# Split-GELU-multiply on one core: VectorE's implied waits dropped, and output tiles fixed instead of rotating

## The chip, the cores and the metric

The kernel runs on 1 core of one Trainium2 chip. The metric is the device time of one execution in microseconds (us); lower is better. A run is timed as a whole; the profile covers a span of it, which is 1.8 us shorter here.

## The reference

The input `x` is float32 of shape (32, 512, 2048), which is 16,384 rows. Each row is split in halves, and the output is GELU of the first half times the second half:

```python
half_dim = x.shape[-1] // 2
x1, x2 = x[..., :half_dim], x[..., half_dim:]
gelu_x1 = 0.5 * x1 * (1 + erf(x1 / np.sqrt(2)))
return (gelu_x1 * x2).astype(np.float32)
```

134.22 MB are read and 67.11 MB written, with one GELU and one product per output element.

## The kernel before

The rows are cut into 16 tiles of 128 partitions by 8 rows. A tile of `x` takes 64 KiB of each partition and a tile of output 32 KiB. Both come from pools with two buffers each. Loads run on the sync engine's queue, two tiles ahead. ScalarE writes GELU into the output tile, VectorE multiplies it in place, and the store is issued from ScalarE's queue (those of the last two tiles from the sync engine's). The first and the last tile are cut in three pieces, the 14 others in two (5 rows and 3 rows).

```python
    xpool = ctx.enter_context(tc.tile_pool(name="xpool", bufs=2))
    opool = ctx.enter_context(tc.tile_pool(name="opool", bufs=2))
    # ... load(i) takes a tile of xpool and starts its DMA; store(...) starts a DMA out ...
    ahead = [load(0), load(1)]
    for i in range(n_tiles):
        x_tile = ahead.pop(0)
        o_tile = opool.tile([P, R, half], out.dtype, name="o_tile")
        # ... last, pieces ...
        steps = ((0, 2), (2, 4), (4, 8)) if pieces else ((0, 5), (5, 8))
        for lo, hi in steps:
            rows = slice(lo, hi)
            tc.keep_in_program_order(
                nc.scalar.activation(out=o_tile[:, rows, :], in_=x_tile[:, rows, :half], func=GELU)
            )
            nc.vector.tensor_mul(
                out=o_tile[:, rows, :], in0=o_tile[:, rows, :], in1=x_tile[:, rows, half:]
            )
            # ... stores of the first and last tile, by halves ...
        if not pieces:
            store(nc.sync if i == n_tiles - 2 else nc.scalar, i, o_tile, slice(0, R))
        if i + 2 < n_tiles:
            ahead.append(load(i + 2))
```

The semaphores are placed by the tile framework. It makes the multiply wait for everything that it depends on: the GELU, the load of `x_tile`, the store that last used the output buffer, and the multiply before that. ScalarE had to wait for the load and the store too, before it began the GELU.

Of the kernel before, what the change touches and what calls it, by code (L numbers as in the profile page):

```python
# [1 line left out]

# [4 lines left out]

GELU = mybir.ActivationFunctionType.Gelu


@with_exitstack
def kernel(
    ctx: ExitStack,
    tc: tile.TileContext,
    x: bass.AP,
    out: bass.AP,
):








    nc = tc.nc
    P = nc.NUM_PARTITIONS

    x_flat = x.flatten_outer_dims()
    out_flat = out.flatten_outer_dims()  # L30
    n_rows, dim = x_flat.shape
    half = dim // 2

    R = 8
    x_t = x_flat.rearrange("(n p r) d -> n p r d", p=P, r=R)
    o_t = out_flat.rearrange("(n p r) d -> n p r d", p=P, r=R)
    n_tiles = x_t.shape[0]

    xpool = ctx.enter_context(tc.tile_pool(name="xpool", bufs=2))
    opool = ctx.enter_context(tc.tile_pool(name="opool", bufs=2))  # L40

    def load(i):
        x_tile = xpool.tile([P, R, dim], x.dtype, name="x_tile")
        for rows in (slice(0, 4), slice(4, 8)) if i == 0 else (slice(0, 8),):
            nc.sync.dma_start(out=x_tile[:, rows, :], in_=x_t[i][:, rows, :])  # L45
        return x_tile

    def store(queue, i, o_tile, rows):
        queue.dma_start(out=o_t[i][:, rows, :], in_=o_tile[:, rows, :])

    ahead = [load(0), load(1)]
    for i in range(n_tiles):
        x_tile = ahead.pop(0)
        o_tile = opool.tile([P, R, half], out.dtype, name="o_tile")
        last = i == n_tiles - 1
        pieces = i == 0 or last
        steps = ((0, 2), (2, 4), (4, 8)) if pieces else ((0, 5), (5, 8))
        for lo, hi in steps:
            rows = slice(lo, hi)
            tc.keep_in_program_order(  # L60
                nc.scalar.activation(  # L61
                    out=o_tile[:, rows, :], in_=x_tile[:, rows, :half], func=GELU
                )
            )
            nc.vector.tensor_mul(  # L65
                out=o_tile[:, rows, :],
                in0=o_tile[:, rows, :],
                in1=x_tile[:, rows, half:],
            )
            if pieces and hi % 4 == 0:  # L70
                store(nc.sync if last else nc.scalar, i, o_tile, slice(hi - 4, hi))
        if not pieces:
            store(nc.sync if i == n_tiles - 2 else nc.scalar, i, o_tile, slice(0, R))
        if i + 2 < n_tiles:
            ahead.append(load(i + 2))


# [1 line left out]
_INS = ['x']  # L79
_OUTS = [((32, 512, 1024), 'float32')]  # L80


# [23 lines left out]
```

## Time and profile before

| What | Value |
|---|---|
| Time, median (range) of the first 3 runs | 470.94 us (470.83 to 471.09) |
| Span of the profile | 469.1 us |
| DMA rate over the span | 429 GB/s |
| VectorE busy, ScalarE busy | 30%, 25% |
| Multiplies, separate wait instructions before them | 34, 31 |

The prediction shows the main lines and reads them. The page lists for each DMA queue its packets, MB and share of 16 engines' time, and for each kind of DMA issue its count, size and median us from issue to landing:

```profile
q14 instruction: 2, 0.02, 0.0%
...
out_dram<-o_tile ACTq DMA_DIRECT2D x13, 4096.0 KB, 44.7
```

The first line says that two packets in the span carried the program's own instructions. The trace has both as 8,192 bytes, at 453.6 and 453.7 us, and 0.309 us long. The second line says that a 4 MB store takes 44.7 us to land.

### The profile page before, as it was taken

Reading aid. Unit: us, or ns where it says so; the run is one execution under the profiler, and the core shown is the slowest. Engines: PE = TensorE matmul, PEld = TensorE weight load, DVE = VectorE, ACT = ScalarE, POOL = GpSimd, SP = SyncE. Lnnn points to the kernel's source line nnn. Section 1 sums busy time; section 2 is a strip of 40 time slices with the busy share of each in tenths; the row PEclk is TensorE's granted clock in tenths of the full one; section 3 lists DMA queues with packets and bytes.
Section 4 is the critical chain, followed back from the end, with each engine's and each line's share of the span. In section 5 each row is a group of like instructions: output and inputs, shape, how many; then the busy total and the mean of one; then the engine's idle time right before and its main releaser. Section 6 shows DMA issues by size and latency. Waiting matters only on the chain.

```text
span 469.1 us, 210 instructions
## 1 busy us (share of the span) xinstructions
DVE 140.5 (30%) x34; ACT 115.5 (25%) x35; POOL 0.2 (0%) x4
## 2 busy tenths in 40 slices
DVE  0330515206051160611506025070240703407052
ACT  1420606041060410505005050140601406023060
POOL 0000000000000000000000000000000000000000
DMA  8999999999999999999999999999999999999998
GB/s 358 447 447 447 414 391 492 402 402 447 492 402 402 447 469 425 402 447 425 469 402 430 419 492 402 402 447 492 402 402 447 469 425 402 447 425 469 402 412 349
DMA packets 5042, 201.35 MB, mean 429 GB/s; under 512 B 560, under 2 KB 560, under 8 KB 560
## 3 DMA queue, kind: packets, MB, share of 16 engines
q1 hardware_dynamic: 2880, 142.61, 70.4%
q10 hardware_dynamic: 2160, 58.72, 29.0%
q14 instruction: 2, 0.02, 0.0%
HBM read 134.22 MB, written 67.11 MB: 429 GB/s over the span
## 4 chain that ended last, share of the span: by engine, by line
DMA 75%; DVE 14%; ACT 8%; ACTq 0%; issue 0%; SPq 0%
DMA out_dram<-o_tile 66%; DVE o_tile L65 14%; DMA x_tile<-in_x_dram 10%; ACT o_tile L61 8%; ACTq L101 0%; SPq L45 0%
## 5 line engine op out<-in xcount | busy, mean ns | idle before, releaser
L65 DVE TENSOR_TENSOR o_tile<-o_tile,x_tile 128x5120 f32<-128x5120 f32 (+3 forms) x34 | 140.5, 4171 | 319.9 <-ACT o_tile L61 319.9
L61 ACT ACTIVATE o_tile<-x_tile 128x5120 f32<-128x5120 f32 (+3 forms) x34 | 114.3, 3407 | 339.6 <-DMA out_dram<-o_tile 301.8
L61 ACT ACT_TABLE_LOAD x1 | 1.3, 1283 | 0.7 <-PEq L90 0.7
L90 POOL MEMSET const-bfloat16-1.0<- 128x1 bf16 x1 | 0.1, 101 | 0.0
L90 POOL MEMSET const-uint8-127<- 128x1 uint8 x1 | 0.1, 101 | 0.0
L90 POOL MEMSET const-float32-0.0<- 128x1 f32 x1 | 0.1, 98 | 0.2 <-issue 0.2
L90 POOL MEMSET const-float32-1.0<- 128x1 f32 x1 | 0.1, 98 | 0.0
## 6 DMA issues: line engine op xcount, KB each, us to landing
out_dram<-o_tile ACTq DMA_DIRECT2D x13, 4096.0 KB, 44.7
x_tile<-in_x_dram SPq DMA_DIRECT2D x2, 4096.0 KB, 16.6
out_dram<-o_tile ACTq DMA_DIRECT2D x2, 2048.0 KB, 34.5
out_dram<-o_tile SPq DMA_DIRECT2D x1, 4096.0 KB, 25.8
out_dram<-o_tile SPq DMA_DIRECT2D x2, 2048.0 KB, 8.0
x_tile<-in_x_dram SPq DMA_DIRECT2D x15, 44.5
```

Source lines behind the costliest of these rows:

```text
L61: nc.scalar.activation(out=o_tile[:, rows, :], in_=x_tile[:, rows, :half], func=GELU)
L65: nc.vector.tensor_mul(out=o_tile[:, rows, :], in0=o_tile[:, rows, :], in1=x_tile[:, rows, half:],)
L90: nc = _bacc.Bacc("TRN2", target_bir_lowering=False, num_devices=1)
```

## The change

The intent: VectorE shall wait for ScalarE alone. What ScalarE waited for before a GELU is done when that GELU is done, so the multiply behind it need not wait for it again. The framework keeps such waits, so they are declared unnecessary. Fixed output tiles make the dependency on the buffer's earlier use one that can be named and dropped; a rotating pool makes that wait itself.

```diff
-    opool = ctx.enter_context(tc.tile_pool(name="opool", bufs=2))
+    opool = ctx.enter_context(tc.tile_pool(name="opool", bufs=1))
+    o_tiles = [opool.tile([P, R, half], out.dtype, name=f"o{k}_tile") for k in range(2)]
 ...
-            nc.sync.dma_start(out=x_tile[:, rows, :], in_=x_t[i][:, rows, :])
+            dma = nc.sync.dma_start(out=x_tile[:, rows, :], in_=x_t[i][:, rows, :])
+            before_gelu[i % 2].append(dma.ins)
 ... (the same in store)
-        o_tile = opool.tile([P, R, half], out.dtype, name="o_tile")
+        o_tile = o_tiles[i % 2]
 ...
-            nc.vector.tensor_mul(
+            mul = nc.vector.tensor_mul(
                 ...
             )
+            for ins in before_gelu[i % 2]:
+                tc.declare_no_dep(mul.ins, ins, reason="ScalarE waited for it")
+            muls.append(mul.ins)
 ...
+        before_gelu[i % 2].extend(muls)
```

More of the change, by code (lines that the diff above doesn't have):

```diff
@@ L44, in load @@
         for rows in (slice(0, 4), slice(4, 8)) if i == 0 else (slice(0, 8),):
-            nc.sync.dma_start(out=x_tile[:, rows, :], in_=x_t[i][:, rows, :])
+            dma = nc.sync.dma_start(out=x_tile[:, rows, :], in_=x_t[i][:, rows, :])
+            before_gelu[i % 2].append(dma.ins)
         return x_tile
     def store(queue, i, o_tile, rows):
-        queue.dma_start(out=o_t[i][:, rows, :], in_=o_tile[:, rows, :])
+        dma = queue.dma_start(out=o_t[i][:, rows, :], in_=o_tile[:, rows, :])
+        before_gelu[i % 2].append(dma.ins)
+    before_gelu = [], []
     ahead = [load(0), load(1)]
@@ L57 @@
         steps = ((0, 2), (2, 4), (4, 8)) if pieces else ((0, 5), (5, 8))
+        muls = []
         for lo, hi in steps:
```

## The prediction

> **What bounds the kernel now.** I read the page's busy shares first, then the waits, then the chain that ended last, then the packets of the DMA queues.
>
> ```profile
> span 469.1 us, 210 instructions
> DVE 140.5 (30%) x34; ACT 115.5 (25%) x35; POOL 0.2 (0%) x4
> ...
> DMA  8999999999999999999999999999999999999998
> ...
> HBM read 134.22 MB, written 67.11 MB: 429 GB/s over the span
> ## 4 chain that ended last, share of the span: by engine, by line
> DMA 75%; DVE 14%; ACT 8%; ACTq 0%; issue 0%; SPq 0%
> ```
>
> VectorE (DVE) works for 30% of the span and ScalarE (ACT) for 25%, while the DMA row stands at 9 in every slice but the first and the last. The chain seems to say something else: it gives VectorE 14% and ScalarE 8%, as if a faster VectorE could shorten the run. It follows waits backwards, from each GELU to the store that freed its buffer, from that store to the multiply, and so on. It does not ask whether the DMA engines were working beside the compute pieces. The table of busy time by stretch does. Its columns are the stretch in us and its length, busy time and count for DVE, ACT and POOL, the clock, the DMA share and the rate; the second stretch holds eight tiles.
>
> ```profile
> 100.48:129.48 29.00, 8.76 (x2) 7.12 (x2) 0.00 (x0) 1.00 1.00 434
> 158.48:390.48 232.00, 70.09 (x16) 56.98 (x16) 0.00 (x0) 1.00 1.00 434
> ```
>
> A tile is 8 MB in and 4 MB out, 12.58 MB in decimal units, and 12.58 MB / 29.00 us = 434 GB/s. The mean DMA share over whole periods is 1.00. A single period could still hide a hole in its compute part, so I laid the packet records over the span myself, each split between the stretches it touches: 100.48 to 113.78 us, where ScalarE and VectorE work on a tile, has a share of 1.00, and 113.78 to 129.48, where both are idle, also 1.00. The first large packet starts 1.75 us into the span and the last ends at 467.77; the share is 1.00 all the way between 3 and 467 us. So **the DMA engines are the bound, with no hole in them**. A typical packet, 32,768 bytes in 1.213 us, is 27.0 GB/s on one engine and 432 GB/s on sixteen; 201.33 MB at 432 GB/s is 466.0 us, which is what lies between those two packets.
>
> **What the change touches.** It touches the waits of VectorE, so I read who waits for whom, on the engines and on the queue that issues the loads.
>
> ```profile
> DVE o_tile L65 <- ACT o_tile L61: 319.9, 18, 21.1
> ACT o_tile L61 <- DMA out_dram<-o_tile: 301.8, 14, 22.1
> ACT o_tile L61 <- DMA x_tile<-in_x_dram: 37.8, 3, 21.0
> ...
> SPq L45 <- DMA x_tile<-in_x_dram: 214.1, 14, 20.4
> SPq L45 <- DVE o_tile L65: 182.6, 14, 13.5
> ```
>
> All of VectorE's idle time, 319.9 us, ends with ScalarE's GELU; none of it ends with a DMA. The waits on DMAs are ScalarE's, 301.8 + 37.8 us. VectorE waits for these DMAs too, in separate instructions, but by the time the GELU is done they are long satisfied. The instructions of the multiply's line between 71 and 77 us show one case (count, shortest, median and longest ns, first and last start):
>
> ```profile
> L65 DVEq EVENT_SEMAPHORE  x2: 50/50/50, 71.5 to 71.6; - x2
> L65 DVE TENSOR_TENSOR o_tile<-o_tile,x_tile x1: 5493/5493/5493, 76.1 to 76.1; 128x5120 f32<-128x5120 f32 x1
> ```
>
> and the timeline around it (start, length, what, idle time before):
>
> ```profile
> 71.56 7.12 ACT L61 ACTIVATE o_tile<-x_tile 128x5120 f32<-128x5120 f32 x2 [17.31 <-DMA out_dram<-o_tile]
> 76.06 8.76 DVE L65 TENSOR_TENSOR o_tile<-o_tile,x_tile 128x5120 f32<-128x5120 f32 x2 [15.67 <-ACT o_tile L61]
> ```
>
> Both wait instructions run as the GELU starts, at 71.5 and 71.6 us, and are over at about 71.66. The multiply starts at 76.06, when the first GELU (4.47 us) has ended at 76.03. The waits have some 4.4 us to spare.
>
> **What the Trainium skill says.** (1) "Perfetto Trace Analysis", section Identifying Dependency Chains: an instruction that waits on several engines may get EventSemaphore instructions put before it for the further waits. The trace agrees: the multiply's line has 34 multiplies and 31 EVENT_SEMAPHORE, and these 31 are what the change takes out. (2) The same page, section Per-engine timelines, on a DVE or Act instruction: it is pushed into a wait queue, waits there for its semaphores, and only its execution is what the profile calls the instruction. That fits the 0.03 us between the GELU's end and the multiply's start, with the sequencer's waits already behind it. (3) "VectorE: DVE Perf Modes", The DRAIN you can't avoid: eight copies took 13.88 us with a semaphore after each and the same with one after the last alone, so semaphores between operations cost nothing there. Nothing in this trace shows a cost either: the second multiply of a tile follows the first without a gap (5.49 + 3.35 = 8.84 us of work in a span of 8.76). (4) The first page again, Roofline: a core alone is bounded by its 16 DMA engines, about 435 GB/s. The trace has 434 in the steady stretch, so no room is left there.
>
> **The change part by part.** The order of instructions and the waits of the built programs were compared engine by engine; no time is in that.
>
> Removed: the 31 EVENT_SEMAPHORE in front of multiplies (one for the first piece, for the third and for tile 1, then two for each of the 14 tiles after, 3 + 28 = 31). In the trace they take 21 or 50 ns each, at most 31 x 50 ns = 1.55 us in all. On the path that sets the end: 0, since each is done about 4.4 us (1.6 to 3.6 us for the pieces of the first and the last tile) before the GELU that the multiply needs anyway.
>
> Unchanged: the 34 multiplies, 34 GELUs and 35 DMA issues stand in the same order with the same shapes, every multiply still waits for ScalarE, ScalarE keeps all its waits for loads and stores, and the sync engine's waits before each load are the same in number and kind.
>
> Moved: the two fixed output tiles lie at the same two addresses that the rotating pool used in turn, and tile i uses buffer i mod 2 as before. Nothing is added: a buffer is refilled when its store has landed, and ScalarE still waits for that.
>
> Sum on the path: 0 from waits, 0 from buffers. Suppose against this that every removed wait had delayed its multiply by its whole length. A multiply that ends 0.1 us earlier lets the store and the load after next be issued 0.1 us earlier, behind transfers that have not finished: load 3 was issued at 60.41 us and its landing took about 44.5 us, where its 8.39 MB alone need 19.4 us at 432 GB/s. The DMA engines have no hole that the earlier issue could fill, so the gain would be spent in the queue. Only the last multiply has transfers behind it that could end earlier, and even there the last store waits behind two others: compute ends at 460.4 us, the DMA at 467.8. So 470.94 + 0 = **470.9 us**.
>
> **The rivals.** *(A) The waits do cost, tile after tile.* The chain of compute and store per buffer is closed: 13.3 us from GELU to the end of the multiplies and 44.7 us to landing make 58.0 us, two tiles' period. If the landing time were fixed, 0.071 us saved per tile (21 + 50 ns, the usual pair) would be worth about 16 x 0.071 = 1.1 us, 0.2%, and the time would be 469.8. Against it: the wait instructions run beside the GELU, and 44.7 us is a queueing time, far over the 9.7 us that 4.19 MB need. *(B) VectorE gets ahead, and earlier issues change how loads and stores mix.* If something moved by a few us, the last store could land later or earlier by some part of one 2 MB piece, which is 4.9 us at 432 GB/s; the range would be 466 to 476. For it: loads and stores share the same engines. Against it: VectorE cannot get ahead, because the GELU's semaphore is the last of its waits in all 18 cases of the waits view. *(C) The fixed buffers bring a new wait,* as when a release of the tile pool had been finer than a buffer dependency: a GELU that waited for a multiply or a store more would lengthen a tile by up to 8.8 us and the run by up to 30%. For it: a pool and a fixed tile are not tracked in the same way. Against it: the built program has the same waits on ScalarE and on the sync engine, row by row.
>
> **Range and chances.** The three runs of before spread over 0.26 us. The mean is set by the bytes and the packet rate, which the change does not touch, so I take a few times that spread for another chip and session: 470.2 to 471.6. (A) alone would fall a little below it, and I give it a tenth. Faster by over 2% would need 461.5 us, under the 466 us that the packets need: 0.01, for an error in this reading. Slower by over 2%, 480.4 us, needs (C) or something that I haven't seen: 0.01. Within 2%: 0.98.
>
> **What would show it.** Right: the EVENT_SEMAPHORE of the multiply's line are gone and the instruction count is 210 - 31 = 179; VectorE's idle time still ends with ScalarE alone, near 320 us over 18 times; the timeline repeats to some 0.05 us, with a period of 29.0 us; the steady rate is 434 GB/s. Step "the waits are hidden" is wrong if the gap between GELU's end and multiply's start falls below 0.03 us. Step "the DMA has no hole" is wrong if the period shrinks below 28.9 us. The prediction falls if ScalarE waits for something else, or if a period grows.

## The result

| Kernel | Runs | Median (range), us |
|---|---|---|
| before | 6 | 470.94 (470.79 to 471.09) |
| changed | 6 | 470.63 (470.49 to 470.87) |

The ratio is 0.9994, 95% interval 0.9981 to 1.0006: the same. Ratios here are the mean time of one kernel's fast runs over that of the other's of the same rounds, so not quite the ratio of the medians quoted.

The page of the changed kernel, with the parts that answer to those shown of before:

```profile
span 469.1 us, 179 instructions
DVE 140.5 (30%) x34; ACT 115.5 (25%) x35; POOL 0.2 (0%) x4
...
q14 instruction: 1, 0.01, 0.0%
HBM read 134.22 MB, written 67.11 MB: 429 GB/s over the span
...
DMA 75%; DVE 14%; ACT 8%; ACTq 0%; issue 0%; SPq 0%
```

The instruction count fell from 210 to 179, which is the 31 wait instructions. Busy times, rate and chain stand as before. Of the lines shown one differs otherwise: one packet of instructions instead of two, at 453.7 us. The busy time by stretch of the changed kernel, with the columns as in the prediction:

```profile
100.48:129.48 29.00, 8.76 (x2) 7.12 (x2) 0.00 (x0) 1.00 1.00 434
158.48:390.48 232.00, 70.08 (x16) 56.98 (x16) 0.00 (x0) 1.00 1.00 434
```

The rate is still 434 GB/s, and tiles take 29.0 us; the length of a stretch is chosen, so what it shows is the count of pieces and the rate. (Later in this execution single tiles take up to 29.1 us; more on that under the prediction.) Who waited for whom in the changed kernel, in total us, times and longest:

```profile
DVE o_tile L75 <- ACT o_tile L71: 320.4, 18, 20.9
ACT o_tile L71 <- DMA out_dram<-o_tile: 302.4, 14, 22.0
...
SPq L49 <- DVE o_tile L75: 182.9, 14, 13.5
```

VectorE's idle time hasn't shrunk, 320.4 us after 319.9. And its timeline at the tile that the prediction showed:

```profile
71.58 7.12 ACT L71 ACTIVATE o_tile<-x_tile 128x5120 f32<-128x5120 f32 x2 [17.37 <-DMA out_dram<-o_tile]
76.08 8.76 DVE L75 TENSOR_TENSOR o_tile<-o_tile,x_tile 128x5120 f32<-128x5120 f32 x2 [15.73 <-ACT o_tile L71]
```

The multiply starts 4.50 us after its GELU starts, as before (76.06 - 71.56). No wait instruction of the multiply's line is left there.

### The profile page after: what moved, and what is told of

It reads as the page before. It is cut to its first block, busy times and chain, and to the rows that moved or that the text cites. A ratio compares the mean times of both kernels' runs of the same rounds, so it can differ in the third digit from the quotient of the medians.

```text
span 469.1 us, 179 instructions
## 1 busy us (share of the span) xinstructions
DVE 140.5 (30%) x34; ACT 115.5 (25%) x35; POOL 0.2 (0%) x4
## 4 chain that ended last, share of the span: by engine, by line
DMA 75%; DVE 14%; ACT 8%; ACTq 0%; issue 0%; SPq 0%
DMA out_dram<-o_tile 66%; DVE o_tile L75 14%; DMA x_tile<-in_x_dram 10%; ACT o_tile L71 8%; ACTq L115 0%; SPq L49 0%
## 5 line engine op out<-in xcount | busy, mean ns | idle before, releaser
L75 DVE TENSOR_TENSOR o_tile<-o_tile,x_tile 128x5120 f32<-128x5120 f32 (+3 forms) x34 | 140.5, 4171 | 320.4 <-ACT o_tile L71 320.4
```

The lines of the kernel that those rows point to most:

```text
L75: mul = nc.vector.tensor_mul(out=o_tile[:, rows, :], in0=o_tile[:, rows, :], in1=x_tile[:, rows, half:],)
```

## The experiments

Two questions were put. The main one is whether the reason is the one predicted: the waits run beside the GELU, and the DMA engines leave no room anyway. The other is where the small difference of 0.3 us comes from. **Theory 1**: waits hidden, DMA the bound. **Theory 2**: each removed wait counts. **Theory 3**: a block of instructions less is fetched. Eleven runs were made in four groups, each group on one chip with the kernel before beside it.

### Each half of the change alone

The changed kernel was run once more as a yardstick:

> The changed kernel once more, with its two halves beside it on the same chip. Its first 6 runs were 0.3 us (0.07%) under the kernel before, with an interval that includes no difference. Theory 1 (the waits are hidden beside the GELU and the DMA engines have no hole): the same as before, a ratio of 0.9990 to 1.0010. Theory 2 (each removed wait counted, 1.1 us in all): 469.8 us, a ratio of 0.9977. Theory 3 (the small difference is real, from one block of 8 KB of VectorE's instructions that is fetched near the end in before, at 453.6 us, and not here): 470.6 us, a ratio of 0.9994, in every kernel with one such fetch at the end, and 470.9 in those with two.

Measured: 470.65 us (470.57 to 470.76, 5 runs) against 470.86 us of before (470.71 to 471.00, 9 runs), ratio 0.9996 (0.9984 to 1.0009).

The fixed tiles alone are the changed kernel without the declarations:

```diff
-            for ins in before_gelu[i % 2]:
-                tc.declare_no_dep(mul.ins, ins, reason="ScalarE waited for it")
```

> The two fixed output tiles alone: the declarations are taken out, so that VectorE has 20 separate wait instructions in front of its multiplies instead of 31 in before and 0 in the changed kernel. Theory 1: ratio 0.9990 to 1.0010. Theory 2 (waits counted one by one): 0.4 us under before, a ratio of 0.9992. A new wait from the fixed buffers (a rival of the prediction): ScalarE's idle time would grow above 340 us. Theory 3: as many fetches at the end as the trace shows decide between 470.6 and 470.9 us.

Measured: 470.90 us (470.80 to 471.16), ratio 1.0003 (0.9989 to 1.0017). The wait instructions of the multiply's line in this kernel (count; shortest, median, longest ns; first and last start):

```profile
L75 DVEq EVENT_SEMAPHORE  x20: 21/182/227, 12.7 to 452.7; - x20
```

20 waits are left, and half of them take 182 ns or more, up to 227 ns. ScalarE's idle time on DMAs is 302.2 + 37.7 us, as before, so the fixed buffers brought no new wait.

The declarations alone keep the rotating pool:

```diff
-    opool = ctx.enter_context(tc.tile_pool(name="opool", bufs=1))
-    o_tiles = [opool.tile([P, R, half], out.dtype, name=f"o{k}_tile") for k in range(2)]
+    opool = ctx.enter_context(tc.tile_pool(name="opool", bufs=2))
 ...
-        o_tile = o_tiles[i % 2]
+        o_tile = opool.tile([P, R, half], out.dtype, name="o_tile")
```

> The dropped waits alone, with the rotating pool of before: 15 separate wait instructions remain on VectorE, because those that come from the pool's reuse of a buffer cannot be declared away. Theory 1: ratio 0.9990 to 1.0010, multiplies still 0.03 us behind their GELU. Theory 2: 0.5 us under before, ratio 0.9989. Theory 3: 470.6 us with one fetch at the end, 470.9 with two.

Measured: 470.91 us (470.81 to 471.07), ratio 1.0002 (0.9989 to 1.0014). 15 waits are left, those that come with the pool's reuse of a buffer.

In one point my wording of theory 3 was loose: the changed kernel has a fetch at 453.7 us too, and before has two there. Whose instructions a fetch carries, the trace doesn't say.

What follows: with 31, 20, 15 and 0 waits the times are 470.86, 470.90, 470.91 and 470.65 us. They don't fall with the number of waits, as theory 2 would have it; its 469.8 us for none is far outside the runs. Theory 1 holds to 0.1%. The 0.2 us of the changed kernel came back in its second set of runs, and neither half has it. Theory 3 as I had put it failed as well: the trace of the declarations alone has one late fetch, and yet it takes 470.9 us and not 470.6. I come back to this below.

### Is the DMA the bound, or the chain?

The chain that ended last puts 14% on VectorE. If the chain were the bound, work added to it would show in the time. In the 14 middle tiles a maximum of the output with itself (which leaves the values, so the result is correct) was put behind the multiplies:

```diff
             muls.append(mul.ins)
+            for _ in range(0 if pieces else 1):    # 2 in the second kernel
+                same = nc.vector.tensor_max(
+                    out=o_tile[:, rows, :], in0=o_tile[:, rows, :], in1=o_tile[:, rows, :]
+                )
+                for ins in before_gelu[i % 2]:
+                    tc.declare_no_dep(same.ins, ins, reason="ScalarE waited for it")
+                muls.append(same.ins)
```

> The changed kernel with VectorE made slower: in the 14 middle tiles a maximum of the output with itself follows the multiplies, 5.49 + 3.35 = 8.84 us more per tile before the store and the next load can be issued. Theory 1 (the DMA engines are the bound and always have work queued): the compute part of a tile grows from 13.3 to 22.1 us, still under the 29.0 us period, so the time stays at 470 to 472 us, although 124 us of work was put into the chain that ended last. Rival (the chain of compute and store is the bound, as its 14% VectorE would have it, with a fixed landing time of 44.7 us): a buffer's period grows from 58.0 to 66.8 us, the run by 7 x 8.84 = 62 us to 533 us.

Measured: 470.90 us (470.86 to 471.03, 4 runs) against 470.99 us (470.73 to 471.18, 7 runs) of before, ratio 0.9999 (0.9984 to 1.0013). The busy time in the same stretch of eight tiles, and the landing of the stores:

```profile
158.48:390.48 232.00, 139.44 (x32) 56.91 (x16) 0.00 (x0) 1.00 1.00 434
...
out_dram<-o_tile ACTq DMA_DIRECT2D x13, 4096.0 KB, 36.0
```

VectorE's work doubled, from 70.1 to 139.4 us in 232, and the rate stayed at 434 GB/s. The tiles took 28.96 to 29.06 us each, but for one of 29.76 us that the last group explains in part. The store was issued some 8.7 us later and landed after 36.0 us instead of 44.7. The 44.7 us was queueing, and the added work was taken out of it. The rival's 533 us is refuted.

> The same with two such maxima per tile, 17.7 us more: the compute part is 31.0 us, and with the issue of the store between two tiles about 31.4 us, over the 29.0 us period. Theory 1: now, and not before, compute becomes the bound; 14 x 2.4 = 34 us more, 495 to 510 us, with a DMA share under 1 in the steady stretch. Rival (fixed landing time): 7 x 17.7 = 124 us more, 595 us. If it stays at 471, VectorE's place in the order is looser than I read.

Measured: 506.65 us (506.47 to 506.76), ratio 1.0757 (1.0739 to 1.0775). Here the waits, the busy time in the same stretch, and two lines of the timeline:

```profile
ACT o_tile L71 <- DVE o_tile L84: 287.4, 12, 24.0
...
158.48:390.48 232.00, 196.45 (x46) 50.12 (x15) 0.00 (x0) 1.00 0.99 407
...
172.71 7.12 ACT L71 ACTIVATE o_tile<-x_tile 128x5120 f32<-128x5120 f32 x2 [23.95 <-DVE o_tile L84]
...
203.78 7.12 ACT L71 ACTIVATE o_tile<-x_tile 128x5120 f32<-128x5120 f32 x2 [23.95 <-DVE o_tile L84]
```

ScalarE now waits for VectorE 12 times instead of for stores, and the period is 203.78 - 172.71 = 31.07 us. A compute part over 29.0 us shows. The DMA share, which I had expected to fall under 1, is still 0.99, though the rate fell to 407 GB/s: by the packet records the loads' packets of 65,536 bytes took 2.57 us in the mean (100 to 400 us), where those of before took 2.418. So a share near 1.00 doesn't tell by itself that the DMA engines are the bound; the rate and the added work do. The 35.7 us more are not simply 14 x 2.07 = 29 us: VectorE is through with tile 14 only at 483.0 us, the DMA share between 468 and 483 us is 0.01, and the stores of the last two tiles, 8.39 MB or 19.4 us at 432 GB/s, come after that (483.0 + 19.4 = 502.4; the last packet ends at 503.6). So the room on the compute side ends somewhere between 22.0 us per tile, the compute part of the kernel with one maximum, and 31 us.

The other direction is a compute part made shorter, by four pieces per middle tile:

```diff
-        steps = ((0, 2), (2, 4), (4, 8)) if pieces else ((0, 5), (5, 8))
+        steps = ((0, 2), (2, 4), (4, 8)) if pieces else ((0, 2), (2, 4), (4, 6), (6, 8))
```

> The changed kernel with a shorter compute part: the middle tiles in four pieces of 2 rows instead of 5 and 3, so VectorE starts after 1.9 us of GELU instead of 4.5, and a tile's compute takes 1.9 + 4 x 2.29 = 11.1 us instead of 13.3. Theory 1: no gain, 470 to 471.5 us, and the landing time of a store grows from 44.7 to about 46.9 us in its place. Rival (chain with a fixed landing time): 7 x 2.2 = 15 us less, 455 us, which would be under the 466 us that the packets take.

Measured: 470.97 us (470.87 to 471.25), ratio 1.0000 (0.9985 to 1.0015). The landing of its stores:

```profile
out_dram<-o_tile ACTq DMA_DIRECT2D x13, 4096.0 KB, 47.1
```

The store is issued some 2.4 us earlier and takes 2.4 us longer to land. What the chain gains, the queue takes back. A gain from the dropped waits would have gone the same way.

### Would the waits cost where compute is the bound?

To see the waits without the DMA limit, two kernels with a wrong result were run. From tile 2 on, a load brings one row of eight, and the middle stores write one row of eight, so most of the output is never written. Input tiles are fixed too. The two differ in VectorE's 19 separate waits alone.

```diff
-        for rows in (slice(0, 4), slice(4, 8)) if i == 0 else (slice(0, 8),):
+        for rows in (slice(0, 4), slice(4, 8)) if i == 0 else (slice(0, 8 if i == 1 else 1),):
 ...
-            store(nc.sync if i == n_tiles - 2 else nc.scalar, i, o_tile, slice(0, R))
+            store(nc.sync if i == n_tiles - 2 else nc.scalar, i, o_tile, slice(0, 1))
```

> A kernel with a wrong result on purpose that takes the DMA engines out of the way: fixed input and output tiles, loads of tiles 2 to 15 and stores of tiles 1 to 14 move one row of eight. The output is therefore wrong. VectorE keeps the waits on loads and stores (19 separate wait instructions). Compute is the bound: about 47 us to the first full tiles, then 4.5 + 8.8 + 0.4 = 13.7 us per tile, some 250 us in all. This run and the next differ in those 19 waits alone. Theory 1 (they run beside the GELU): the two agree within 0.2 us. Theory 2 (each on the path): this one is 14 x 0.05 to 0.07 = 0.7 to 1 us longer, 0.3 to 0.4%.

> The same kernel with a wrong result on purpose, with the declarations of the changed kernel, so that VectorE waits for ScalarE alone (no separate wait instruction). Theory 1: as long as the run with the waits, within 0.2 us, and the multiply starts 0.02 to 0.03 us behind its GELU in both. Theory 2: 0.7 to 1 us shorter, with a multiply that starts nearer to its GELU.

Measured: 215.58 us (215.50 to 215.71, 4 runs) with the waits and 215.22 us (215.19 to 215.29, 5 runs) without. One period with the waits:

```profile
109.66 0.36 ACTq L55 DMA_DIRECT2D out_dram<-o_tile  x1
110.12 7.12 ACT L72 ACTIVATE o_tile<-x_tile 128x5120 f32<-128x5120 f32 x2 [3.37 <-DVE o_tile L76]
114.63 8.76 DVE L76 TENSOR_TENSOR o_tile<-o_tile,x_tile 128x5120 f32<-128x5120 f32 x2 [1.73 <-ACT o_tile L72]
120.15 0.36 ACTq L55 DMA_DIRECT2D out_dram<-o_tile  x1
```

and without them:

```profile
109.75 0.36 ACTq L55 DMA_DIRECT2D out_dram<-o_tile  x1
110.22 7.12 ACT L72 ACTIVATE o_tile<-x_tile 128x5120 f32<-128x5120 f32 x2 [3.37 <-DVE o_tile L76]
114.72 8.76 DVE L76 TENSOR_TENSOR o_tile<-o_tile,x_tile 128x5120 f32<-128x5120 f32 x2 [1.73 <-ACT o_tile L72]
120.25 0.36 ACTq L55 DMA_DIRECT2D out_dram<-o_tile  x1
```

The periods are 10.49 and 10.50 us, and the multiply starts 4.51 and 4.50 us after its GELU starts. My 13.7 us per tile was a miss: the store of the first row waits for the first multiply alone, so ScalarE begins the next tile while VectorE is at the second piece. That doesn't touch the comparison. The waits cost nothing here either, where compute is the bound (DMA share 0.47 between 100 and 155 us) and where GELU is still the last thing that a multiply waits for. A multiply whose separate wait ends last was not tried. The two differ by 0.36 us all the same, more than the 0.2 us that I had allowed. The mean span is 213.50 with the waits and 213.42 us without; the other 0.28 us lie outside the span, in 2.09 against 1.81 us (each run's time minus its span). The traces differ there in one packet: with the waits, a fetch of 8,192 bytes starts at 215.2 us, behind the span's end at 213.4, and without them there is none.

### Where the last 0.2 us come from

The light kernels gave the hint: time is a span plus a part outside it, and they must be read apart. The run records have both. Theory 3 was refined so, and tested on the changed kernel with tiny memsets of a scratch column as fillers, which are instructions of VectorE and not waits:

```diff
+    scratch = fpool.tile([P, 64], x.dtype, name="scratch")
+    columns = iter(range(31))    # 20 in the other kernel
 ...
+        for _, f in zip(range(2), columns):
+            tc.keep_in_program_order(nc.vector.memset(scratch[:, f : f + 1], 0.0))
         for lo, hi in steps:
```

> The changed kernel beside the two kernels with fillers, on the same chip. What is left to explain is 0.2 to 0.3 us. Theory 3 in its refined form: the time is a span and a part outside it; inside the span the number of 8 KB instruction fetches counts (each takes 0.31 us of a DMA engine that has no hole), outside it a fetch in the closing program costs 0.26 to 0.4 us. This kernel has one fetch inside and none just after: span 468.9, outside 1.78, time 470.65, as in its first two runs.

> The changed kernel, with no separate waits on VectorE, but with 31 tiny memsets of a scratch column in front of the multiplies: as many VectorE instructions as before. Theory 3 refined: two late fetches in the span as in the kernel before, span 469.1, outside 1.79, time 470.9, the same as before. If instead the dropped waits themselves make the 0.2 to 0.3 us, this kernel stays at 470.65 us, as the changed kernel.

> The same with 20 fillers, as many VectorE instructions as the kernel with the fixed tiles alone. Theory 3 refined: one late fetch in the span and one just after it: span 468.9, outside 2.05, time 470.95. If the waits themselves count: 470.65 us with 1.79 outside.

Measured medians: changed 470.62 us (470.55 to 470.70), 31 fillers 471.07 us (470.99 to 471.29), 20 fillers 470.89 us (470.81 to 471.00), all of 5 runs; before 470.87 us (470.70 to 471.01, 9 runs). Ratios to before: 0.9995 (0.9982 to 1.0007), 1.0005 (0.9991 to 1.0019) and 1.0001 (0.9988 to 1.0013). The queue of instructions on the page with 31 fillers:

```profile
span 469.2 us, 210 instructions
...
q14 instruction: 2, 0.02, 0.0%
```

This table has the means of the runs, and the late fetches of 8,192 bytes in each profiled execution. VectorE's records are those in its trace. The row of before takes its means from the runs of this last group; on the chips of the first two groups its mean span was 469.07 and 469.19 us.

| Kernel | VectorE records | Fetches in the span, after it | Span, us | Outside, us | Time, us |
|---|---|---|---|---|---|
| changed (third set) | 40 | 1, 0 | 468.84 | 1.78 | 470.62 |
| declarations alone | 55 | 1, 0 seen | 468.74 | 2.19 | 470.93 |
| fixed tiles alone | 60 | 1, 1 | 468.92 | 2.04 | 470.96 |
| changed + 20 fillers | 60 | 1, 1 | 468.86 | 2.04 | 470.90 |
| four pieces | 68 | 2, 0 | 469.25 | 1.77 | 471.01 |
| one maximum more | 68 | 2, 0 | 469.12 | 1.80 | 470.92 |
| before | 71 | 2, 0 | 469.09 | 1.78 | 470.87 |
| changed + 31 fillers | 71 | 2, 0 | 469.30 | 1.78 | 471.08 |

The kernels fall into two groups. With one fetch in the span, the mean spans are 468.74 to 468.92 us; with two, 469.09 to 469.30. Outside the span it's 1.77 to 1.80 us, but 2.04 where a fetch falls just behind the span (at 470.65 and 470.69 us in the traces). Single executions don't sort so cleanly: the first profiled one of the changed kernel had one fetch and a span of 469.1 us.

The fillers help to decide between waits and instructions. 20 of them, with no wait, gave the pair of numbers of the fixed tiles alone: the span of the changed kernel (468.86 against 468.84 us) and 0.26 us more outside. 31 took the gain away, and more: 471.07 us is 0.2 us above the 470.9 that I expected and above before. What that excess is was not found. A cost of the fillers' own would hardly show with 31 alone, when 20 add 0.02 us to the span. So the 0.2 to 0.3 us of the changed kernel are most likely no saving of waits; it has 31 instructions less to fetch.

A delay that goes with a fetch can be seen where one falls into the middle of a run; a tile's time runs from the start of its first GELU to that of the next tile's:

| Kernel | Fetch starts at, us | Tile it falls in, us | Other tiles from 100 to 420 us |
|---|---|---|---|
| 31 fillers | 317.2 | 29.64 | 28.98 to 29.01 |
| one maximum more | 346.1 | 29.76 | 28.96 to 29.06 |
| four pieces | 309.8; 342.5 | 29.29; 29.41 | 28.98 to 29.01 |

These tiles are 0.3 to 0.8 us longer, by about the fetch's own 0.309 us or more. Why it can be more, and why the mean spans are only 0.3 to 0.5 us over that of the changed kernel, is not shown. Open is also why the declarations alone have 2.19 us outside without a fetch in the records: it may come after the trace ends. And no single ratio here excludes 1; the split rests on 4 to 9 runs per kernel that spread over 0.15 to 0.38 us.

## Why the prediction was right

- **"The DMA engines are the bound, with no hole in them."** Right. 8.7 us of added compute per tile changed the time by nothing, a compute part shorter by 2.4 us changed nothing, and only over the period did it show (31.07 us per tile). The landing times of the stores, 36.0, 44.7 and 47.1 us, gave and took what compute took and gave, to 0.1 us. Of the evidence it rested on, the DMA share of 1.00 was the weak part: the share is 0.99 with two maxima, where compute sets the period.
- **"On the path that sets the end: 0" for the waits.** Right. The kernels with 0, 15 and 20 waits are within 0.1% of the one with 31, and with the DMA limit taken away the period stays 10.5 us with and without them. The gap between GELU's end and the first multiply of a middle tile is 0.03 us in all of them.
- **Buffers: nothing added, nothing moved.** Right. Fixed tiles alone: ratio 1.0003, and ScalarE's waits unchanged. Rival (C) did not happen.
- **Rival (A), 469.8 us**, did not happen, and the fixed landing time that it needs was refuted. **Rival (B)**: VectorE got nowhere ahead, 320.4 us idle over 18 waits for ScalarE.
- **The size.** 470.9 was predicted and 470.63 measured, inside the range. The 0.27 us that the sum misses are most likely a term it didn't have: the fetch of instructions. The prediction counted the removed instructions' time and not their bytes.
- **"The timeline repeats to some 0.05 us"** was too narrow. It does so up to 187.5 us; then tiles of up to 29.11 us follow in the changed kernel, and at the last tile GELU starts at 448.69 in one trace and 449.17 us in the other, while both spans end at 469.1. A growing period was named as a sign against the prediction. It isn't one of the change: in the next two traces of the changed kernel these tiles take 28.97 to 29.04 us. The drifting execution was the slowest of its six (470.87 us); what the drift cost is not shown.

## What to carry to other kernels

Waits that were satisfied before the last wait of the same instruction were free here, one or two in front of a multiply; look for the wait that ends last, and change that. A share in the chain that ended last is no proof of a bound, and neither is a DMA share near 1: add work to the chain once, and if the landing time of the DMAs shrinks by as much and the rate stays, it's the DMA engines that set the time. When 0.05% is at stake, split the time into the span and the part outside, and count the fetched blocks of instructions before crediting the edit itself.

## What the Trainium skill lacked or had wrong

- "Runtime: NRT & Kernel Launch", section Instruction fetch mechanics, says that instructions are refilled in blocks of 16 KiB and that crossing a boundary is mostly hidden. The traces show fetches as packets of 8,192 bytes, one of which comes alone. Where the DMA engines are full, kernels with a second one in the span have mean spans 0.2 to 0.6 us longer, a tile with one in it is 0.3 to 0.8 us longer, and one just behind the span goes with 0.26 us more outside it.
- "DMA: Bandwidth & Descriptors", section Where 436 GB/s comes from, says that for transfers between HBM and SBUF the HBM side, about 358 GB/s, binds. With one core at work it didn't: loads and stores together ran at 434 GB/s for 232 us. The passage doesn't name the case; the section Roofline that the prediction cites does, and agrees with the 434.
- No page I read says when the extra wait instructions cost time. Here they took 21 to 50 ns in the kernel before and up to 227 ns with fixed tiles alone, and no cost showed in either place; the wait for ScalarE ended 1.6 to 4.5 us later in before.
